# Cutting one store of the last group into four transfers in a matmul + bias + residual kernel

## The chip, the cores and the metric

The kernel runs on one core of a Trainium2 chip. The core has five engines that run their own instruction streams: PE (matrix multiply), DVE (VectorE), ACT (ScalarE), POOL (GpSimd) and SP (SyncE, which only issues transfers here). Sixteen DMA engines move data between HBM and the on-chip memory SBUF, which has 128 partitions. The metric is the device time of one execution in microseconds; lower is better.

## The reference

```python
x:        (16, 512, 1024) float32
weight:   (1024, 768)     float32
bias:     (768,)          float32
residual: (16, 512, 768)  float32
out = (np.matmul(x, weight) + bias + residual).astype(np.float32)
```

With the first two dimensions flattened this is one product of 8192 x 1024 by 1024 x 768. It reads 61.9 MB and writes 25.2 MB.

## The kernel before

The 8192 rows are cut into 8 groups of 1024 (`n_grp`), and a group into 8 tiles of 128 rows (`G = 8`). Partition `p` of a group holds its rows `8p` to `8p + 7`, so that a store of tiles `j0` to `j1` writes, for each partition, one unbroken run of `(j1 - j0) * 768 * 4` bytes: 24,576 bytes for a whole group, 12,288 for half of one.

Two tiles of a group's half are handled together by each engine. ACT casts x to bf16 (`cast_x`, L119), DVE and ACT transpose it in 32 x 32 blocks (L143, L149, L124), PE multiplies (L295) into the four PSUM buffers of `po`, and DVE adds the product onto the residual in place in SBUF (`evacuate`, L155; two tiles at a time, in the last group's last quarter one at a time). POOL then adds the bias to the same place (`add_bias`, L197), for the last pair of tiles ahead of the rest. What has both is stored from there.

All transfers, loads and stores, are issued by SP in one written order, so they also stand in one queue, in this order:

```python
ORDER = ("x0a w0 bias w1 x0b r0 x1a x1b r1 x2 r2 x3 r3 x4 st0 st1 "
         "r4 x5 r5 st2 x6a x6b r6 x7a x7b r7 st3 st4+ st6 st7a st7b st7c").split()
LAST_PARTS = {"a": (0, 4), "b": (4, 6), "c": (6, 8)}
```

`x`, `w` and `r` are loads of x, weight and residual, `st` are stores; a digit is the group, `st4+` stores groups 4 and 5 at once. The last group's store is in three parts: `st7a` holds tiles 0 to 3 (12,288 bytes in each of 128 partitions, 1536 KB), `st7b` and `st7c` two tiles each (6,144 bytes a partition, 768 KB). Before each name SP waits for what the transfer needs: for `st7a` and `st7b` the POOL adds of their last tiles (L259), for `st7c` the last DVE add (L257). The transfer itself is L267.

Stores from group 3 on count on one semaphore, `st`: each transfer adds 16 when it is through. `late` (L34) is the sum over them. It is added by ACT before the critical section and taken off again at its start (L35, L127), and SP's last instruction (L38) waits until the count reaches `late`, which is when every late store has landed.

Of the kernel before, what the change touches and what calls it, by code (L numbers as in the profile page):

```python
# [10 lines left out]
P = 128  # L11
# [4 lines left out]
ORDER = ("x0a w0 bias w1 x0b r0 x1a x1b r1 x2 r2 x3 r3 x4 st0 st1 "  # L16
         "r4 x5 r5 st2 x6a x6b r6 x7a x7b r7 st3 st4+ st6 st7a st7b st7c").split()
PARTS = {"": (0, 8), "a": (0, 4), "b": (4, 8)}
LAST_PARTS = {"a": (0, 4), "b": (4, 6), "c": (6, 8)}


@with_exitstack
def kernel(
    ctx: ExitStack,
    tc: tile.TileContext,
    x: bass.AP,
    weight: bass.AP,
    bias: bass.AP,
    residual: bass.AP,
    out: bass.AP,  # L30
):
    nc = tc.nc
    stored = ctx.enter_context(nc.semaphore("st"))
    late = 16 * sum(name[:2] == "st" and int(name[2]) > 2 for name in ORDER)  # L34
    nc.scalar.sem_inc(stored, late)  # L35
    with tc.tile_critical(name="all", no_gpsimd_drain=True):  # L36
        emit(nc, ctx, x, weight, bias, residual, out, stored, late)
    nc.sync.wait_ge(stored, late)  # L38


def emit(nc, es, x, weight, bias, residual, out, stored, late):
# [11 lines left out]
    sp, act, dve, pool, pe = nc.sync, nc.scalar, nc.vector, nc.gpsimd, nc.tensor  # L53
# [18 lines left out]
    def sem(name):  # L72
        if name not in sems:
            sems[name] = es.enter_context(nc.semaphore(name))
        return sems[name]

    def wait(eng, name, value):
        eng.wait_ge(sem(name), value)
# [14 lines left out]
    def group(ap, g):  # L93
        return ap[g * G * P:(g + 1) * G * P, :].rearrange("(p j) k -> p j k", p=P)

    def span(start, size):
        return data[:, start:start + size] if isinstance(start, int) else data[:, bass.ds(start, size)]

    def x_rows(g, j, n):
        return span(X0 - (g % 2) * X_SLOT + j * K, n * K).rearrange("p (t k) -> p t k", k=K)  # L100

    def r_home(g):

        return (g % 4) * R_SLOT + ((g + 1) // n_grp) * (X0 - 3 * R_SLOT)

    def r_rows(start, j, n):
        return span(start + j * N, n * N).rearrange("p (j n) -> p j n", n=N)
# [107 lines left out]
    def load_into(name):  # L215

        before = landed.get(name, 0)
        landed[name] = before + 16
        if before:
            wait(sp, name, before)  # L220
        return name

    for name in ORDER:
        into = name
        if name == "bias":
            wait(sp, "ev", EV0)
            src, dst = bias[None, :].to_broadcast((P // Q, N)), bias_rows[0:P:Q, :]
        elif name[0] == "w":
            k0 = int(name[1]) * (R // 2)
            src, dst = w_rows[:, k0:k0 + R // 2, :], w_stage[:, k0:k0 + R // 2, :]  # L230
        elif name[0] == "x":
            g, part = int(name[1]), name[2:]
            j0, j1 = PARTS[part]
            if g > 1 and part != "b":
                wait(sp, "cast", 2 * (2 * g - 2))
            if g == 3:
                wait(sp, "wc", 2)
                whole = 16 * sum(n[0] == "x" and len(n) == 2 for n in ORDER)
                sp.sem_inc(sem("xb"), whole)
                landed["xb"] += whole  # L240
            into = load_into("xb" if part == "b" else "xa")
            src, dst = group(x2d, g)[:, j0:j1, :], x_rows(g, j0, j1 - j0)
        elif name[0] == "r":
            g = int(name[1])
            if g == n_grp - 1:
                wait(sp, "cast", 2 * (2 * g))
            elif g > 3:
                wait(sp, f"st{g - 4}", 16)
            into = load_into("r")
            src, dst = group(res2d, g), r_rows(r_home(g), 0, G)  # L250
        else:
            g, part = int(name[2]), name[3:]
            n = 2 if part == "+" else 1
            j0, j1 = (LAST_PARTS if g == n_grp - 1 else PARTS)[part.strip("+")]
            end = (g + n - 1) * G + j1
            if end == n_sub:
                wait(sp, "ev", ev_end)  # L257
            else:
                wait(sp, "add", added[end - 1])  # L259
            src, dst = r_rows(r_home(g), j0, j1 - j0), group(out2d, g)[:, j0:j1, :]  # L260
            if n > 1:
                src = span(r_home(g), n * R_SLOT).rearrange("p (g k) -> p g k", g=n)
                dst = out2d[g * G * P:(g + n) * G * P, :].rearrange(
                    "(g p j) n -> p g (j n)", g=n, p=P)
            if g > 2:
                into = "st"
        sp.dma_start(out=dst, in_=src).then_inc(sem(into), 16)  # L267

    half_bytes = B * (R // 2) * P * 4
    xt_end = nc.lookup_mloc(xt).addr + (P - 1) * 4  # L270
# [16 lines left out]
    with pe.Fori(0, n_bat):  # L287
        mv.wait()
        tm.wait()
        for i in range(B):  # L290
            if i % 2 == 0:
                ev.wait()
            for k in range(R):
                for c, (n0, nl) in enumerate(chunks):
                    ins = pe.add_instruction(mybir.InstMatmult(  # L295
                        name=nc.get_next_instruction_name(),
# [38 lines left out]
```

## Time and profile before

| | us |
|---|---|
| median of 3 runs | 209.47 (209.45 to 209.48) |
| the profiled execution's own time | 209.74 |
| its span, first to last instruction | 208.0 |
| PE busy | 171.1 (82%) |
| DVE busy | 166.4 (80%) |
| ACT busy | 144.8 (70%) |
| POOL busy | 115.5 (56%) |
| DMA: share of sixteen engines' span | 97.9% |
| DMA: bytes moved | 87.05 MB, 419 GB/s over the span |

Busy time is the time in which an engine executes instructions; it is an average over the span, and says little of the last microseconds, in which only stores are left. Times in the views of the trace count from the first instruction. The DMA rows of the page give the mean over sixteen engines, so that one engine alone is a share of 0.06.

### The profile page before, as it was taken

The page shows a single profiled execution, that of the slowest core. Times are in us where ns is not written, and L with a number is a line of the kernel's source. Part 1 is how long each engine was busy: PE and PEld are TensorE (multiplying, and loading weights), DVE is VectorE, ACT ScalarE, POOL GpSimd, SP SyncE. Part 2 cuts the span into 40 slices and gives each one's busy share as a digit, 9 for nine tenths or more (in the row PEclk, how much of TensorE's full clock was granted, in tenths as well). Part 3 has the DMA queues.
Part 4 walks back from the last instruction along what each step waited for, and adds up shares of the span by engine and source line. Part 5 has one row for each costly group of instructions (what it writes and reads, how often), then busy time and mean ns, then how long its engine had stood idle before and what let it go on. Part 6 is the DMA issues. An engine that isn't in the chain of part 4 may idle for free.

```text
span 208.0 us, 2388 instructions
## 1 busy us (share of the span) xinstructions
PE 171.1 (82%) x1024; PEld 50.6 (24%) x512; DVE 166.4 (80%) x180; ACT 144.8 (70%) x162; POOL 115.5 (56%) x38
## 2 busy tenths in 40 slices
PE   0000999969998999999999999599999999999910
PEld 0000232313232333232322333122323232233300
DVE  1068497899889989999999968995999999994510
ACT  2367975997599696979697669888497969750000
POOL 0055006639391939293938484484809393999910
PEclk9999999999999999999999999789999999999985
DMA  6999999999999899999999999999999999999994
GB/s 208 429 433 433 440 425 419 449 465 429 405 421 479 380 440 429 449 416 421 449 449 413 427 425 449 407 448 416 444 410 470 391 444 449 411 430 444 421 408 169
DMA packets 4600, 87.05 MB, mean 419 GB/s; under 512 B 500, under 2 KB 500, under 8 KB 760
## 3 DMA queue, kind: packets, MB, share of 16 engines
q1 hardware_dynamic: 4600, 87.05, 97.9%
HBM read 61.88 MB, written 25.17 MB: 419 GB/s over the span
## 4 chain that ended last, share of the span: by engine, by line
DMA 57%; PE 16%; DVE 12%; issue 5%; ACT 4%; DVEq 0%; SPq 0%; ACTq 0%
DMA data<-in_x_dram 46%; PE po L295 16%; DMA out_dram<-data 11%; DVE xt L149 7%; DVE data L155 3%; ACT xb L119 2%; ACT xt L124 2%; DVE tq L143 2%; SPq L267 0%; DVEq L89 0%; ACTq L89 0%; ACTq L119 0%; DVEq L155 0%; DVEq L162 0%; ACTq L131 0%
## 5 line engine op out<-in xcount | busy, mean ns | idle before, releaser
L295 PE MATMUL po<-w_sb,xt 128*128 128x512 bf16 (+1 forms) x1024 | 171.1, 330 | 27.2 <-DVE xt L149 20.3
L197 POOL TENSOR_TENSOR data<-data,bias_bc 128x1536 f32<-128x1536 f32 x32 | 109.8, 3450 | 69.7 <-DVE data L155 69.6
L124 ACT COPY xt<-tq 32x512 uint32<-32x512 uint32 x128 | 78.9, 617 | 22.4 <-DVE tq L143 19.7
L149 DVE STREAM_TRANSPOSE xt<-xb 32x512 uint32<-32x512 uint32 x128 | 90.1, 704 | 4.8 <-ACT xb L119 2.8
L295 PEld LDWEIGHTS po<-w_sb,xt 128*128 x512 | 50.6, 99 | 147.1 <-issue 146.2
L119 ACT CAST xb<-data 128x2048 bf16 x32 | 64.8, 2073 | 16.9 <-DMA data<-in_x_dram 16.6
L155 DVE TENSOR_TENSOR data<-po,data 128x1536 f32 (+2 forms) x33 | 55.9, 1708 | 11.1 <-PE po L295 10.7
L143 DVE STREAM_TRANSPOSE tq<-xb 128x1024 uint32<-128x1024 uint32 x16 | 19.8, 1237 | 5.4 <-ACT xb L119 5.4
L192 POOL CAST w_sb<-data 128x3072 bf16<-128x3072 f32 x2 | 5.5, 2744 | 12.9 <-DMA data<-in_weight_dram 12.9
L160 DVE LOAD_MASK_SELECT bias_bc<-bias_rows x1 | 0.0, 14 | 10.3 <-DMA bias_rows<-in_bias_dram 10.3
L128 ACT ACT_TABLE_LOAD x1 | 1.3, 1283 | 1.0 <-SPq L36 1.0
L157 DVE MEMSET bias_rows<- 128x768 f32 x1 | 0.7, 698 | 1.2 <-SPq L36 1.2
L160 DVE STREAM_SHUFFLE bias_bc<-bias_rows 128x768 f32<-128x768 f32 x1 | 1.0, 1006 | 0.0
L319 POOL MEMSET const-float32-0.0<- 128x1 f32 x1 | 0.1, 98 | 0.2 <-issue 0.2
L128 ACT COPY warm<-const-float32-0.0 128x1 f32<-128x1 f32 x1 | 0.2, 191 | 0.0
L319 POOL MEMSET const-bfloat16-1.0<- 128x1 bf16 x1 | 0.1, 102 | 0.0
L319 POOL MEMSET const-uint8-127<- 128x1 uint8 x1 | 0.1, 102 | 0.0
L319 POOL MEMSET const-float32-1.0<- 128x1 f32 x1 | 0.1, 98 | 0.0
## 6 DMA issues: line engine op xcount, KB each, us to landing
data<-in_residual_dram SPq DMA_DIRECT2D x8, 3072.0 KB, 17.0
data<-in_x_dram SPq DMA_DIRECT2D x8, 2048.0 KB, 17.5
data<-in_x_dram SPq DMA_DIRECT2D x4, 4096.0 KB, 19.4
out_dram<-data SPq DMA_DIRECT2D x5, 3072.0 KB, 23.9
out_dram<-data SPq DMA_DIRECT2D x1, 6144.0 KB, 29.5
data<-in_weight_dram SPq DMA_DIRECT2D x2, 1536.0 KB, 12.1
out_dram<-data SPq DMA_DIRECT2D x1, 1536.0 KB, 8.6
out_dram<-data SPq DMA_DIRECT2D x2, 768.0 KB, 7.3
```

The costliest lines, as they stand in the source:

```text
L119: act.copy(out=xb[:, c], in_=part.rearrange("p t (a j r) -> p t j a r", j=R // 2, r=2)).then_inc(sem("cast"), 1)
L124: act.copy(out=xt[q * Q:(q + 1) * Q, half, :, :, m * Q:(m + 1) * Q], in_=tq[m * Q:(m + 1) * Q, :, :, q]).then_inc(sem("mv"), 1)
L128: act.copy(out=warm[:], in_=nc.const_aps.tensor(0.0, [P, 1], FP32))
L143: dve.transpose(out=tq[:], in_=xb_words(0)).then_inc(sem("tq"), 1)
L149: ins = dve.transpose(out=xt[q * Q:(q + 1) * Q, half, :, :, m * Q:(m + 1) * Q], in_=words[m * Q:(m + 1) * Q])
L155: dve.tensor_add(out=rt, in0=po[:, j % 4:j % 4 + n, :N], in1=rt).then_inc(sem("ev"), 1)
L157: dve.memset(bias_rows[:], 0.0).then_inc(sem("ev"), EV0)
L160: dve.stream_shuffle(out=bias_bc[:], in_=bias_rows[:], mask=[0] * 32).then_inc(sem("bb"), 1)
L192: pool.tensor_copy(out=w_sb[:, part, :], in_=w_stage[:, part, :]).then_inc(sem("wc"), 1)
L197: pool.tensor_add(out=rt, in0=rt, in1=bias_bc[:, None, :].to_broadcast((P, 2, N))).then_inc(sem("add"), 1)
L295: ins = pe.add_instruction(mybir.InstMatmult(name=nc.get_next_instruction_name(), ins=[pe.lower_ap(w_sb[:, k, n0:n0 + nl]), stationary(i, k)],
L319: nc = _bacc.Bacc("TRN2", target_bir_lowering=False, num_devices=1)
```

## The change

`st7a`, until now one transfer of 128 partitions, goes as four: partitions 0 to 111, 112 to 118, 119 to 125, and 126 and 127, one issued after the other in the place that `st7a` had. The bytes, their addresses and all other transfers stay as they are. Each of the four adds 16 to `st`, so that `late` counts nine transfers instead of six (144 instead of 96).

```diff
+PIECES = {"a": (0, 112, 119, 126, 128)}
+
+
+def pieces(name):
+    cuts = PIECES[name[3:]] if name[:3] == "st7" and name[3:] in PIECES else (0, P)
+    return list(zip(cuts, cuts[1:]))
...
-    late = 16 * sum(name[:2] == "st" and int(name[2]) > 2 for name in ORDER)
+    late = 16 * sum(len(pieces(name)) for name in ORDER if name[:2] == "st" and int(name[2]) > 2)
...
-        sp.dma_start(out=dst, in_=src).then_inc(sem(into), 16)
+        for p0, p1 in pieces(name):
+            if p1 - p0 < P:
+                sp.dma_start(out=dst[p0:p1], in_=src[p0:p1]).then_inc(sem(into), 16)
+            else:
+                sp.dma_start(out=dst, in_=src).then_inc(sem(into), 16)
```

## The prediction

> **What bounds the kernel now.** I read the page from the top, then the waits of SP, the end of the span in short windows, the order of SP and POOL there, and last the trace's DMA records (one per packet: start, duration, bytes) and its landings (one per engine and transfer).
>
> ```profile
> span 208.0 us, 2388 instructions
> ...
> DMA  6999999999999899999999999999999999999994
> GB/s 208 429 433 433 440 425 419 449 465 429 405 421 479 380 440 429 449 416 421 449 449 413 427 425 449 407 448 416 444 410 470 391 444 449 411 430 444 421 408 169
> ...
> q1 hardware_dynamic: 4600, 87.05, 97.9%
> ...
> out_dram<-data SPq DMA_DIRECT2D x1, 1536.0 KB, 8.6
> out_dram<-data SPq DMA_DIRECT2D x2, 768.0 KB, 7.3
> ```
>
> The DMA engines are full in every slice but the first and the last (97.9% of sixteen engines' span), at 419 GB/s; no compute engine is over 82%. So bytes set the time, and the 1536 KB store in the last lines, st7a, is the one cut up. The program then waits for the last landing:
>
> ```profile
> SPq L36 <- DMA out_dram<-data: 7.2, 1, 7.2
> ```
>
> What it waits for shows in the last microseconds, in the columns after PEclk (DMA share, GB/s):
>
> ```profile
> 204.00:204.50 0.50, 0.00 (x0) 0.00 (x0) 0.00 (x0) 0.00 (x0) 0.00 (x0) 0.50 1.02 430
> 204.50:205.00 0.50, 0.00 (x0) 0.00 (x0) 0.00 (x0) 0.00 (x0) 0.00 (x0) 0.50 0.40 160
> 205.00:205.50 0.50, 0.00 (x0) 0.00 (x0) 0.00 (x0) 0.00 (x0) 0.00 (x0) 0.50 0.09 37
> 205.50:206.00 0.50, 0.00 (x0) 0.00 (x0) 0.00 (x0) 0.00 (x0) 0.00 (x0) 0.50 0.09 37
> 206.00:206.50 0.50, 0.00 (x0) 0.00 (x0) 0.00 (x0) 0.00 (x0) 0.00 (x0) 0.50 0.06 25
> ```
>
> The share drops from 1.02 to 0.09, and one engine in sixteen is 0.06: nearly all stop together and one goes on. Packets of one engine follow back to back (the next starts 4 ns before the last ends), so they can be strung into sixteen chains. The median chain ends at 204.83, one ("the second") at 205.30, and the last ("the late engine") at 206.66; it lands at 207.13, and the span ends 0.82 after that. The late engine's lag on the median grows in stores alone: 0.68 us after st1, 0.95 after st2, 1.16 after st3, 1.60 after st4+, 1.78 after st6, 1.83 after st7a and at the end.
>
> **The change part by part.** The rows stay the same, 128 of 12,288 bytes. In the records a row takes 460 ns and starts 456.5 ns after the one before; I call 0.457 us a row-time.
>
> *Who carries the rows.* Now each engine has 8. That 112 rows lie 7 on each of sixteen follows the records of 128 (8 each); that 7 rows lie one each on seven engines follows the bias load, whose 4 rows are on four engines and give four landings. I take it that small pieces always start at the same first engines. Then engines 0 and 1 carry 7+1+1+1 = 10 rows, engines 2 to 6 carry 9, and nine engines carry 7. The trace doesn't number engines, but neither the late engine nor the second is among the four that carried bias. So of the twelve others the late engine is one of nine that lose a row, or one of three that gain one.
>
> *Freed from the late engine.* It did st7a's 8 rows from 199.25 to 202.95, 0.463 each. One row less: 206.66 becomes 206.20, a gain of 0.46.
>
> *Added to engines 0 and 1.* Two rows, 0.91, and three closing packets of 4 bytes at 6 ns: 204.83 becomes 205.76. That is 0.44 short of the late engine, so it costs nothing if rows keep their price. The cover of the two rows is the lag itself.
>
> *Issue on SP.* Three more DMA instructions, between 0.332 (st7b) and 0.650 us (bias, the only one of few rows): 1.0 to 1.95 us.
>
> ```profile
> 177.19 17.24 POOL L197 TENSOR_TENSOR data<-data,bias_bc 128x1536 f32<-128x1536 f32 x5 [4.05 <-DVE data L155]
> 194.88 3.43 POOL L197 TENSOR_TENSOR data<-data,bias_bc 128x1536 f32<-128x1536 f32 x1 [0.44 <-DVE data L155]
> ```
>
> SP issues st7a when POOL's five adds end, at 194.46, and then sits until POOL's last add ends at 198.31, when st7b goes out. Even at 0.65 each the pieces are out by 196.8, and the first load shows about 1.0 us from issue to first packet: 197.8. The engines come to st7a at 197.47, when st6 is through, and to the first small piece seven row-times later, at 200.7. The added issues cost nothing; nothing behind them on SP starts later. The larger count (144 for 96) is one number in two instructions. No engine's compute waits for st7a.
>
> *What small pieces do to each other: the unknown.* In 128-row transfers no engine seems to hinder another. In the new pieces, engines read neighbouring partitions at once: partitions 112 to 118, then 119 to 125, then 126 and 127. Free, that is three row-times for engine 1 (10 with the 112). The far bound: let eight neighbouring partitions give no more than one engine draws now. The 112 rows then take 8 row-times, and the pieces 7, 6 and 2 after each other: 23 in place of 8, +6.85 us, 211.68 for engine 1, 5.0 after the late engine's 206.66. The nearest row is the bias load, the only transfer of few rows. Its packets are recorded at 121 ns, but they land 0.48, 0.48, 0.55 and 0.62 us after their closing packet, where w0, just before, needs 0.36 to 0.42 on fifteen engines: 0.09 to 0.23 late, which is 0.8 to 2.0 of their 117 ns. And in w1 right after, one chain alone, the second, shows a longer packet at once (504 ns for 460). So a row of a small piece costs 1.8 to 3.0 row-times by it. With 8 for the 112, engine 1 needs 8 + 3 x 1.8 = 13.4 to 8 + 3 x 3.0 = 17: 5.4 to 9 row-times over now, 2.47 to 4.11 us, ending at 207.30 to 208.94: 0.64 to 2.28 after 206.66. I take 2.28, since bias' rows lie 32 partitions apart and the new ones side by side.
>
> [...]
>
> **Sum.** Profiled time 209.74 (span 208.0 and 1.74 around it), plus 2.28: 212.02. The timed median is 0.27 below the profiled run: 211.75, so 211.8.
>
> **The rivals.**
>
> *Relief (the other side).* Rows cost the same in any piece, the late engine is one of the nine, and the end moves by its one row: 209.47 - 0.46 = 209.0. For it: packet records of bias aren't lengthened, and w1's chains besides the second run at 460 ns, which they should not if a shared place were full. Against it: the late landings. It decides as long as engine 1 needs no more than 0.48 us, one row-time, beyond its ten; from 1.3 us on, the kernel is slower. [...]
>
> *Half a hindrance.* Engine 1 loses 0.5 to 1.3 us over its ten rows: its end is between 206.24 and 207.08, the time within 0.42 of now, about 209.5.
>
> *The late engine is given a row.* If it is one of the three, it gets one row more instead of one less: 209.47 + 0.46 = 209.9. By count this is 3 of 12.
>
> *The change doesn't do what it says.* If rows are dealt by partition and not by count, each engine keeps the rows that it has, and only closing packets are added (6 ns each): 209.5. Against it: bias' partitions 0, 32, 64 and 96 went one to each of four engines, though nothing tells where a 128-row transfer puts them.
>
> **How the numbers follow.** A measurement of this kernel tells about 0.2%, 0.42 us, from no change. Hindrance that decides: 0.53, with its own range 210.1 (0.64 over) to 213.0. The far bound, 214.5, supposes that the pieces never overlap, and I leave 0.05 above 213.0. Half a hindrance has 0.06, dealing by partition 0.04. The 0.37 left is free of hindrance, shared by the count of engines, nine to three: relief 0.28, a row more for the late engine 0.09. So faster 0.28, same 0.10, slower 0.62. To hold 8 in 10 the range has to reach down to relief: 208.9 to 213.0.
>
> **What the changed profile would show.** Hindrance: packets of 12,288 bytes well over 460 ns in the 199 to 207 stretch, several engines busy in the last windows (share 0.2 to 0.5 where 0.06 stood), and a final wait of SP over 9 us. Relief: all such packets at 460 ns but the late engine's, its end at 206.2, the share still falling to 0.06 or 0.12 and SP's final wait near 6.7. Issues: SP's last issue still at 199.2. I am wrong if the small rows run at 460 ns, or if the late engine's lag differs in this run: the lag has no cause in the trace but "in stores".

## The result, and the profile after

The changed kernel takes 212.07 us (median of 4 runs, 211.36 to 212.21) against 209.47: a ratio of 1.0117, 95% interval 1.0094 to 1.0140. It is slower by 2.60 us, and 211.8 had been forecast. A second measurement, beside the experiments, gave 212.10 against 209.47, ratio 1.0116 (1.0094 to 1.0137).

The profiled execution took 211.36, the shortest of the four. Its page, in the lines that answer to those shown of before:

```profile
span 209.5 us, 2391 instructions
...
DMA  6999999999999999999999899999999999999992
GB/s 225 421 435 458 399 428 438 450 450 400 428 472 400 425 475 400 403 427 446 441 441 444 380 446 441 419 416 435 432 425 450 436 408 436 446 432 422 413 354 115
...
q1 hardware_dynamic: 4616, 87.05, 97.6%
```

The same bytes, and 16 packets more: the closing packets of the pieces, on 7, 7 and 2 engines. What has changed is the end: the two last slices carry 354 and 115 GB/s, where 408 and 169 stood in slices a little shorter. The end in short windows (columns as before; DMA share and GB/s are the last two):

```profile
204.00:204.50 0.50, 0.00 (x0) 0.00 (x0) 0.00 (x0) 0.00 (x0) 0.00 (x0) 0.50 0.92 369
204.50:205.00 0.50, 0.00 (x0) 0.00 (x0) 0.00 (x0) 0.00 (x0) 0.00 (x0) 0.50 0.77 320
205.00:205.50 0.50, 0.00 (x0) 0.00 (x0) 0.00 (x0) 0.00 (x0) 0.00 (x0) 0.50 0.62 258
205.50:206.00 0.50, 0.00 (x0) 0.00 (x0) 0.00 (x0) 0.00 (x0) 0.00 (x0) 0.50 0.38 160
206.00:206.50 0.50, 0.00 (x0) 0.00 (x0) 0.00 (x0) 0.00 (x0) 0.00 (x0) 0.50 0.24 98
206.50:207.00 0.50, 0.00 (x0) 0.00 (x0) 0.00 (x0) 0.00 (x0) 0.00 (x0) 0.50 0.21 86
207.00:207.50 0.50, 0.00 (x0) 0.00 (x0) 0.00 (x0) 0.00 (x0) 0.00 (x0) 0.50 0.18 74
207.50:208.00 0.50, 0.00 (x0) 0.00 (x0) 0.00 (x0) 0.00 (x0) 0.00 (x0) 0.50 0.12 49
208.00:208.50 0.50, 0.00 (x0) 0.00 (x0) 0.00 (x0) 0.00 (x0) 0.00 (x0) 0.50 0.03 12
```

Before, fifteen engines stopped by 205.3 and one went on alone, a share of 0.06. Now four are still at work at 206.2 (0.24) and two at 207.7 (0.12). Which, the DMA records show. Strung into chains as for the prediction, these four end last in the profiled run. Each line has the rows of 12,288 bytes in ns; `|` is a closing packet with its time; the two stores of 6,144 bytes a row are left out. It is a reading: where two chains meet within some ns, they could be exchanged.

```
|197.42  460 460 460 460 460 460 460 |200.62  969 |201.59 1740 |203.33 460 |203.80   ends 207.50   ten rows
|197.51  460 460 460 460 460 560 825 |201.18 1179 |202.41 1938 |204.35               ends 208.06   nine rows
|197.30  460 460 460 460 460 460 460 |200.50 1344 |201.84  935 |202.78               ends 206.48   nine rows
|198.94  467 464 460 1206 460 460 460 |202.90 460 |203.36 1307 |204.67               ends 208.37   nine rows, the late engine
```

The row of 1179 ns is strung behind the closing packet at 201.18. Behind the one at 201.20, which belongs to a ten-row engine, a row of 460 ns follows at once, as it does after most closing packets; the other way, with two gaps of over 20 ns, the engine that ends at 208.06 would have ten rows. As strung here, the second ten-row engine has all its rows at 460 ns and ends at 205.83.

The rows are dealt as the forecast had it: seven engines take a second and third transfer, two of them a fourth, and nine have 7 rows. Rows of the small pieces take up to 1938 ns, where every row of the same store before took 460 to 494. Some rows of the 112 are longer too, on engines that have no small piece: 1428 and 1214 on one, 1114 on another. And the late engine is among the seven: it has a row more, not less.

### The profile page after: what moved, and what is told of

It reads as the page before. It is cut to its first block, busy times and chain, and to the rows that moved or that the text cites. A ratio compares the mean times of both kernels' runs of the same rounds, so it can differ in the third digit from the quotient of the medians.

```text
span 209.5 us, 2391 instructions
## 1 busy us (share of the span) xinstructions
PE 171.5 (82%) x1024; PEld 50.7 (24%) x512; DVE 166.4 (79%) x180; ACT 144.8 (69%) x162; POOL 115.5 (55%) x38
## 4 chain that ended last, share of the span: by engine, by line
DMA 57%; PE 16%; DVE 12%; issue 5%; ACT 4%; DVEq 0%; SPq 0%; ACTq 0%
DMA data<-in_x_dram 45%; PE po L305 16%; DMA out_dram<-data 11%; DVE xt L155 7%; DVE data L161 3%; ACT xb L125 2%; ACT xt L130 2%; DVE tq L149 2%; SPq L277 0%; DVEq L95 0%; ACTq L95 0%; ACTq L125 0%; DVEq L161 0%; DVEq L168 0%; ACTq L137 0%
```

## The experiments

The count theory says that only the number of rows an engine carries matters. Two theories were tried besides it. *Sharing*: engines that read neighbouring partitions at the same time share what one engine draws. *Number*: four transfers cost more than one, whatever they carry. In the table, each kernel stands beside the kernel before on the same chip. An edit shown is against the changed kernel, those of cols4, extra4 and extra7 are against the kernel before, and that of extra7n is against extra7; `...` marks lines left out.

| kernel | st7a | median us | before | ratio (95%) |
|---|---|---|---|---|
| only112 | 112 alone | 210.68 | 209.41 | 1.0062 (1.0044 to 1.0080) |
| sixteen | 112, 16 | 210.75 | 209.41 | 1.0055 (1.0033 to 1.0076) |
| spread | 112, 7, 7, 2, pieces 4 apart | 211.71 | 209.41 | 1.0098 (1.0077 to 1.0120) |
| cols4 | 4 x 128 of 3072 bytes | 209.54 | 209.41 | 1.0008 (0.9999 to 1.0018) |
| extra4 | 128, then 2 loads of 4 rows | 209.63 | 209.53 | 1.0004 (0.9994 to 1.0013) |
| extra7 | 128, then 2 loads of 7 rows | 210.57 | 209.53 | 1.0050 (1.0033 to 1.0067) |
| quarters | 4 x 32 partitions | 211.52 | 209.53 | 1.0106 (1.0079 to 1.0133) |
| early16 | 128; st0 as 112, 16 | 216.42 | 209.53 | 1.0329 (1.0311 to 1.0346) |
| after_again | 112, 7, 7, 2 | 212.10 | 209.47 | 1.0116 (1.0094 to 1.0137) |
| spread_again | as spread | 211.66 | 209.47 | 1.0099 (1.0084 to 1.0113) |
| spread4x4 | 112, 4, 4, 4, 4, pieces 4 apart | 210.39 | 209.47 | 1.0049 (1.0034 to 1.0063) |
| extra7n | 128, then 2 loads of 7 neighbours | 210.63 | 209.47 | 1.0052 (1.0037 to 1.0066) |

### Not the number of transfers: cols4

```diff
...
+        if name == "st7a":
+            for j in range(4):
+                sp.dma_start(out=dst[:, j:j + 1, :], in_=src[:, j:j + 1, :]).then_inc(sem(into), 16)
...
```

`late` counts the three transfers more.

> st7a as four transfers of 128 partitions, one per tile (3072 bytes a partition in place of 12288), everything else as before. Sharing theory: each engine keeps to its own partitions, 24 more packets and 3 closing packets for the late engine at some 5 ns: 209.5 to 209.7. Theory of the number of transfers: three more, as in the changed kernel: 212.1. Count theory: 209.5.

Four transfers for one, each over all 128 partitions, cost 0.13 us, and all but two of the 512 new packets are recorded at 121 ns. So the number of transfers is not the cause.

### The 112 partitions alone: only112

```diff
-PIECES = {"a": (0, 112, 119, 126, 128)}
+PIECES = {"a": (0, 112)}
```

> st7a stores partitions 0 to 111 alone; the rows of 112 to 127 in the first half of the last group are left out. Sharing theory (engines that read neighbouring partitions at once share what one engine draws): the small pieces did the harm, so without them the late engine is a row short and the time is 209.0; if the 112 rows hinder each other too (the late engine had one of 1206 ns in the changed kernel), up to 209.8. Count theory (only the number of rows an engine carries matters): 209.0. Theory of the number of transfers: 209.0, since one transfer stays one.

This does less work than the kernel before, and no engine has more than 7 rows; it is 1.27 us slower, beyond what any theory said. So the big piece does harm by itself. The end of its profiled run, of 210.14 us:

```profile
204.00:205.00 1.00, 0.00 (x0) 0.00 (x0) 0.00 (x0) 0.00 (x0) 0.00 (x0) 0.50 0.52 215
205.00:206.00 1.00, 0.00 (x0) 0.00 (x0) 0.00 (x0) 0.00 (x0) 0.00 (x0) 0.50 0.15 61
206.00:207.00 1.00, 0.00 (x0) 0.00 (x0) 0.00 (x0) 0.00 (x0) 0.00 (x0) 0.50 0.07 31
207.00:208.00 1.00, 0.00 (x0) 0.00 (x0) 0.00 (x0) 0.00 (x0) 0.00 (x0) 0.50 0.00 0
```

Half of the engines are through at 204.5, early by the row that they don't have, and one is alone from 206.2 on (0.07). It is the late engine: its seven rows are recorded at 460, 460, 460, 740, 460, 631 and 1128 ns and take from 199.16 to 203.49, 4.33 us, where in the kernel before it took 3.71 for eight. Freed of a row it should have gained 0.46; by the medians the kernel lost 1.27. If the late engine ends last in every run, as it does in the profiled one, the division costs it 1.73; in the profiled run, which is 0.54 below the median, its seven rows lost 1.12. The next to last engine lost too: its seven rows end in 562, 664, 926 and 1178 ns.

### The small pieces: spread, and the pair again

```diff
-                sp.dma_start(out=dst[p0:p1], in_=src[p0:p1]).then_inc(sem(into), 16)
+                part = src[p0:p1] if p0 == 0 else src[0:4 * (p1 - p0):4]
+                sp.dma_start(out=dst[p0:p1], in_=part).then_inc(sem(into), 16)
```

> The transfers of the changed kernel, 112, 7, 7 and 2, but the small pieces read partitions 0, 4, 8 and so on (step 4) in place of 112 to 127, so that sixteen rows of the output hold another row's sums; counts, bytes, addresses in HBM and number of transfers are the changed kernel's. Sharing theory: the pieces' rows run at 460 ns; what is left is the late engine's row more (0.46) and what the 112 rows do to it: 209.9 to 210.7. Count theory and theory of the number of transfers: as the changed kernel, 212.1.

The rows of the pieces ran at 460 ns, as the sharing theory said, on all but one of the seven engines (756 and 632). The addresses in HBM are those of the changed kernel, so that the place in SBUF is what made the small rows slow. But the time is 211.71, 1 us over that theory's range, which had put little on the 112 rows. In the run profiled here the late engine's seven took 5.42 us (624, 872, 500, 873, 487, 901, 1152). To see what the place of the pieces is worth, both kernels ran again side by side.

> The changed kernel again, beside the spread one on one chip, for the price of the small pieces' place: 212.1.

> Pieces at partitions 0, 4, 8 and so on, again (output rows 112 to 127 hold other rows' sums). If the small pieces decide, as the prediction had it, the changed kernel is over this one by its hindered rows, 1 us and more. If the 112 rows and the late engine's two more rows decide (the kernel of 112 alone, 1.27 over before with one row of each engine left out, plus two rows, 0.91: 2.2 over before), the two differ by less than 0.5.

212.10 and 211.66: a difference of 0.44 in the medians, with intervals that overlap, so that the place of the pieces is worth little in time and may be worth nothing. In the profiled run of spread_again an engine with seven rows and no piece ends at 208.00 (its last five rows took 1480, 1365, 918, 912 and 1134 ns), 0.72 before the late engine: the 112 rows hold up others too. Here is the end of the changed kernel's run, of 212.32 us:

```profile
205.00:206.00 1.00, 0.00 (x0) 0.00 (x0) 0.00 (x0) 0.00 (x0) 0.00 (x0) 0.50 0.47 184
206.00:207.00 1.00, 0.00 (x0) 0.00 (x0) 0.00 (x0) 0.00 (x0) 0.00 (x0) 0.50 0.28 117
207.00:208.00 1.00, 0.00 (x0) 0.00 (x0) 0.00 (x0) 0.00 (x0) 0.00 (x0) 0.50 0.22 92
208.00:209.00 1.00, 0.00 (x0) 0.00 (x0) 0.00 (x0) 0.00 (x0) 0.00 (x0) 0.50 0.06 25
209.00:210.00 1.00, 0.00 (x0) 0.00 (x0) 0.00 (x0) 0.00 (x0) 0.00 (x0) 0.50 0.02 6
```

The engine alone after 208.2 is not the late one (208.08) but one with ten rows: seven at 460 until 201.18, then 1898, 1948 and 635 ns, ending at 209.37. So two ends compete: in this run the pieces decide, in the first one the late engine did. Spreading the pieces bought so little because the late engine's end did not come earlier: 209.48 and 208.72 in the profiled runs of spread and spread_again.

### 112 and 16: sixteen

```diff
-PIECES = {"a": (0, 112, 119, 126, 128)}
+PIECES = {"a": (0, 112, 128)}
```

> st7a goes as 112 and 16 partitions, so that every engine carries 7 + 1 = 8 rows, as before. Count theory: 209.5. [...] Theory of the number of transfers: half of the way to the changed kernel's three more is less than a third of 2.6 us, under 210.4.

Eight rows for each engine, as before, and still 1.34 slower, where the count theory had no change. In the records the last row takes 460 to 2675 ns on the sixteen engines that read the sixteen neighbours. Yet the late engine ends last again, at 209.06 in the profiled run, which was the longest of the four: its rows of the 112 took 460, 748, 973, 952, 508, 906 and 952 ns, the last one 848. The median is 0.07 above that of 112 alone, though each engine has a row more. In medians of 4 and 8 runs that scatter by 1.6 us each, that says no more than that the two are near.

### Whose row it is: extra4 and extra7

To separate the count of rows from their place, the kernel before was given two more transfers behind an unchanged st7a. They are loads into a part of SBUF that is no longer needed, each to partitions four apart (`MORE` is 4 or 7):

```diff
...
+        if name == "st7a":
+            wait(sp, "cast", 4 * n_grp)
+            for h in (0, 1):
+                rows = x2d[h * 64:h * 64 + 3 * MORE, :].rearrange("(p j) k -> p (j k)", j=3)
+                sp.dma_start(out=data[0:4 * MORE:4, X1 + h * 3 * K:X1 + (h + 1) * 3 * K],
+                             in_=rows).then_inc(sem(into), 16)
```

> The kernel before, with two more transfers behind st7a, each a load of 4 rows of 12288 bytes (of x, into a part of SBUF that is no longer used) to partitions 0, 4, 8 and 12: two rows more on the four engines that carried bias, none on the others, no row of st7a moved. Late engine outside these four: 209.4, since the four end at 205.8. If every engine with more rows delays the end, or more transfers do: 210.3.

> The same with two loads of 7 rows, to partitions 0, 4, up to 24: two rows more on seven engines, as the changed kernel's two pieces of 7 have. Late engine among the seven (as the records of the changed kernel and of the spread one have it): two rows, 0.91 later, 210.3. Late engine among the other nine: 209.4.

Two rows more on four engines cost 0.10, which can't be told from nothing. Two rows more on seven cost 1.04. The windows of extra4 first, then of extra7:

```profile
205.00:206.00 1.00, 0.00 (x0) 0.00 (x0) 0.00 (x0) 0.00 (x0) 0.00 (x0) 0.50 0.28 117
206.00:207.00 1.00, 0.00 (x0) 0.00 (x0) 0.00 (x0) 0.00 (x0) 0.00 (x0) 0.50 0.02 6
```

```profile
205.00:206.00 1.00, 0.00 (x0) 0.00 (x0) 0.00 (x0) 0.00 (x0) 0.00 (x0) 0.50 0.36 147
206.00:207.00 1.00, 0.00 (x0) 0.00 (x0) 0.00 (x0) 0.00 (x0) 0.00 (x0) 0.50 0.07 31
207.00:208.00 1.00, 0.00 (x0) 0.00 (x0) 0.00 (x0) 0.00 (x0) 0.00 (x0) 0.50 0.02 6
```

More engines are busy after 205 in both, and in both one goes on alone; with four rows it ends at 206.44, with seven at 207.44. It is the late engine, which came to st7a 1.4 us and more behind the median in both (199.08 and 199.14), with 8 rows in extra4 and 10 in extra7. So the late engine is one of the seven that small transfers of 7 use, and none of the four that transfers of 4 use.

### Is the late engine's row all that tells spread from 112 alone: spread4x4

```diff
-PIECES = {"a": (0, 112, 119, 126, 128)}
+PIECES = {"a": (0, 112, 116, 120, 124, 128)}
```

with spread's line for the source.

> 112 partitions and four pieces of 4, each reading partitions 0, 4, 8 and 12 (so that output rows 112 to 127 hold other rows' sums): the late engine gets no second or third row, the four first engines get eleven. By sum of the parts: as the kernel of 112 alone, 210.7, since the four end at 206.2 if their rows keep 460 ns. If a piece behind the 112 rows costs something by itself: as the spread one, 211.7.

210.39: near the 210.68 of 112 alone, and 1.27 below spread_again on the same chip. Moving the pieces from the late engine to the four saves its two rows, which extra7 had at 1.04. But the number of pieces is not all that differs. Five transfers kept SP busy for 6.12 us, st7b went out at 200.47 only, and the DMA engines that were through with st7a stood still until 202.0:

```profile
194.31 6.12 SPq L276 DMA_DIRECT2D out_dram<-data  x5
200.47 2.17 SPq L278 DMA_DIRECT2D out_dram<-data  x2
201.00:202.00 1.00, 0.00 (x0) 0.00 (x0) 0.00 (x0) 0.00 (x0) 0.00 (x0) 0.87 0.29 111
```

The late engine was at its seven rows until 203.72, did not have to wait, and ended last at 207.42. Whether the pause of the others made its rows shorter is not shown.

### Other divisions: quarters and early16

```diff
-PIECES = {"a": (0, 112, 119, 126, 128)}
+PIECES = {"a": (0, 32, 64, 96, 128)}
```

> [...] Theory that only the 112 division is bad: 209.5. Number of transfers: refuted by the four of 3072 bytes, 209.5.

2.0 slower, with st7a in four transfers of 32 partitions and eight rows on each engine, so that it is not the division with 112 alone that costs. 30 of the 128 rows take 900 ns or more, up to 1598 (939, 949, 991 and 1229 in turn on one engine). 67 rows stay at 460 to 467. Here the late engine is spared (460 to 504 ns a row) and ends at 206.41, before most of the others: the engines that are in step hinder each other, and the last of them ends at 208.18.

```diff
-PIECES = {"a": (0, 112, 119, 126, 128)}
+PIECES = {"st0": (0, 112, 128)}
...
-    cuts = PIECES[name[3:]] if name[:3] == "st7" and name[3:] in PIECES else (0, P)
+    cuts = PIECES.get(name, (0, P))
...
-                wait(sp, f"st{g - 4}", 16)
+                wait(sp, f"st{g - 4}", 16 * len(pieces(f"st{g - 4}")))
```

> The division 112 and 16 of the kernel sixteen put on the first store, st0 (rows of 24576 bytes), where the late engine is 0.4 us behind and not 1.8; st7a as before. If what the late engine loses in the division comes from being out of step (the others have gone on to rows of 128-partition transfers, which it then asks for beside them): little, 209.4 to 209.9. If the division costs in step too: rows are twice as long, 2 x 1.3 us: 212, or whatever part of it is made up before the end.

216.42: 6.9 slower, more than either side had expected. That a division hurts only an engine out of step is refuted here as in quarters. The windows of early16, then those of before:

```profile
90.00:95.00 5.00, 5.00 (x33) 1.52 (x16) 4.90 (x7) 3.79 (x7) 5.00 (x2) 1.00 1.26 393
95.00:100.00 5.00, 4.95 (x32) 1.52 (x16) 4.49 (x5) 4.95 (x4) 1.45 (x2) 1.00 0.74 236
```

```profile
90.00:95.00 5.00, 5.00 (x33) 1.54 (x16) 4.90 (x8) 3.66 (x7) 5.00 (x2) 1.00 0.98 423
95.00:100.00 5.00, 5.00 (x33) 1.47 (x15) 4.49 (x5) 4.93 (x5) 1.46 (x2) 1.00 1.03 442
```

A row of 24,576 bytes, 912 ns before, is recorded at up to 5996 ns, and the load r4 waits until st0 has landed. SP's timeline of early16 and of before:

```profile
101.79 0.36 SPq L277 DMA_DIRECT2D data<-in_residual_dram  x1
```

```profile
96.33 0.34 SPq L267 DMA_DIRECT2D data<-in_residual_dram  x1
```

It goes out 5.5 us later, and the DMA engines that are through have little to do meanwhile (236 GB/s for 442). At the end of the program, where nothing stands behind the store, the same division costs 1.34.

### Neighbours among loads: extra7n

```diff
-                sp.dma_start(out=data[0:4 * MORE:4, X1 + h * 3 * K:X1 + (h + 1) * 3 * K],
+                sp.dma_start(out=data[h * MORE:(h + 1) * MORE, X1 + h * 3 * K:X1 + (h + 1) * 3 * K],
```

> The kernel with two more loads of 7 rows, but to neighbouring partitions (0 to 6, then 7 to 13) in place of every fourth; all else as there. [...] If place does not matter: 210.6 and rows of 460.

The time is close to that of extra7, 210.63: the late engine, which comes when the others are done, still ends last (207.65). The records differ as sharing has it, but a row late: the first row is at 460 or 461 on six engines and 614 on the seventh, the second at 605 to 1178 on all seven. The bias load was like that: its packets are recorded at 121 ns and landed 0.48 to 0.62 us after their closing packet, where w0 needed 0.36 to 0.42. Why a row that is held up shows late is not shown.

## Why the prediction was right, and where it was not

*What bounds the kernel; the late engine.* Right. Its lag on the median was there in every run, and what was added to it came out at the end (extra7), what was added to others did not (extra4).

*Who carries the rows.* Right: 10, 9 and 7. But "one of nine that lose a row, or one of three that gain one" was weighed by number, and it is one of the three (8 rows in extra4, 10 in extra7). Relief was never to be had: with rows at 460 ns throughout, the change would have cost one row, 0.46.

*Small rows at 1.8 to 3.0 row-times.* Right in kind, and on the mean in size: the sixteen rows of the pieces took 2.0 row-times on the mean in the first run (904 ns) and 2.2 in the second (1000 ns). But the sum took 3.0 for each of engine 1's three. The ten-row engines, as strung above, took 460 + 460 + 460 and 969 + 1740 + 460 ns in the first run, 1216 + 1216 + 500 and 1898 + 1948 + 635 in the second: 1.0, 2.3, 2.1 and 3.3 row-times a row. They ended at 205.83, 207.50, 207.67 and 209.37; the forecast was 208.94. The late landings of the bias load were a usable price. Its unlengthened packets, which I had put down for relief, were a poor sign, as extra7n suggests.

*The 112 partitions at 8 row-times for engine 1, nothing for the late engine.* This step failed. The 8 rested on a supposition, that eight neighbouring partitions give no more than one engine draws, and no run shows that bound. The ten-row engines' seven rows were clean in both runs (460 each, as strung). The late engine, which had been given a gain of 0.46, got a row more and was held up besides. In the changed kernel's two profiled runs its rows of the 112 took 0.76 and 0.13 us longer than seven at 460 ns, and its two small rows (460 + 1307, 561 + 1432) 0.85 and 1.07 longer than two. So it ended at 208.37 and 208.08, 1.71 and 1.42 later than before. "Engine 1 decides by its three small rows" is half of the truth: in the second run a ten-row engine ended last, in the first the late engine did.

The medians seem to add up: only112 measures 1.27, two rows cost 1.04 by extra7, that makes 2.3, and spread measures 2.30 and 2.19. The 0.3 to 0.4 that the changed kernel takes beyond that would be the pieces' place. But its own records divide otherwise: the late engine lost 1.1 to 2.3 us in the 112 rows in the profiled runs of only112, sixteen and the three spread kernels, and no more than 0.76 in those of the changed kernel. So the total is measured, and what each part adds to it differs from run to run.

*The number.* That 211.8 came so near 212.07 is in part luck. The total was worked out for engine 1, and in the first run it was reached by the late engine, from which the sum had taken a row away where one was added, and whose hold-up it had put at nothing. The range, 208.9 to 213.0, held relief and hindrance alike, so that a time within it favours neither.

*Issue on SP.* The bound was wrong, and the cover held in the changed kernel. The pieces behind the first took 0.73, 1.09 and 1.20 us of SP, not 0.33 to 0.65, and the last store 2.6 instead of 0.33:

```profile
194.14 3.50 SPq L275 DMA_DIRECT2D out_dram<-data  x4
198.03 3.53 SPq L277 DMA_DIRECT2D out_dram<-data  x2
```

SP's last issue ended at 201.56 and not by 199.6, so that its final wait was shorter than forecast, not longer:

```profile
SPq L42 <- DMA out_dram<-data: 6.8, 1, 6.8
```

The first engine came to st7c at 202.49, so nothing waited for it. In spread4x4 the cover did not hold, as shown above, and in spread_again some engines stood still for up to 0.6 us before st7c, whose issue ended at 202.60; the late engine was still at its earlier rows in both.

*The place in SBUF.* The rows of the pieces were priced at the upper end because they lie side by side, and place did matter: small rows at up to 1948 ns ran at 460 on six of seven engines when they were read four partitions apart (spread). How much neighbouring rows hold each other up is not one number: the ten-row engines took 7 row-times for the 112 rows and 3.0 to 9.8 for the rest, 10 to 17 in all.

What stays open: which partitions each engine takes of 112, and with it why engines in step mostly run them at 460 ns and the late one does not; the records name neither engine nor partition. That engines meet at neighbouring partitions is shown for the pieces, by spread; for the 112 rows it is argued, and no run tells SBUF from HBM there. Nor is it known why the late engine falls behind in stores. A division that would relieve it without engines meeting was not tried.

## What to carry to other kernels

Transfers that each run over all 128 partitions were worth more here than an even count of rows. In st7a, the cut by columns cost 0.13 us, while the three divisions of the same bytes by partitions, two of them with equal counts, cost 1.3 to 2.6 us there; 112 and 16 cost 6.9 on the first store, where a load waited behind it. Before work is moved off a late engine, find out by added rows which engines a small transfer uses (loads of four rows cost 0.10 us here, loads of seven 1.04), because the small transfer may land on the late one. And read landings beside packet records: the hold-up of the small loads here showed in their landings (bias, 0.48 to 0.62 us after the closing packet) or in the next packet (605 to 1178 ns in extra7n), mostly not in their own (121 ns in bias; in extra7n the first row was at 460 or 461 on six of seven engines).

## What the runs showed of the hardware that was not expected

- Two ends that compete hide each other's price: taking away the place of the pieces saved 0.44 at most by the medians, though single rows were up to 1.5 us longer than 460 ns (1948).
- A store of 112 partitions, which leaves out an eighth of st7a, was slower than the whole one (210.68 against 209.41).
- SP's issue of a transfer took 0.33 or 0.34 us when it stood alone (0.39 for the first load, 0.40 for st4+) and 0.40 to 0.79 right behind another in the kernel before. The pieces behind the first took 0.67 to 1.95, and the last store up to 3.1 in runs in which rows were held up (spread_again); where rows ran at 460 ns, in extra4, it took 0.33.
- Divisions by partitions scatter: 210.77 to 212.56 in the changed kernel's second measurement and 209.94 to 211.57 with 112 alone, where the kernel before stays within 209.41 to 209.62 beside the first.
